# Layer norms and block sums without GpSimd: the norm's affine part as two VectorE steps, 96 GpSimd subtractions and additions moved to VectorE

## The chip, the core and the metric

The kernel runs on one core of one Trainium2 chip. The metric is the device time of one launch in microseconds (us); the time of a kernel is the median of several runs. The engines are named as in the profile: PE is TensorE (matrix products and transposes), DVE is VectorE, ACT is ScalarE, POOL is GpSimd, SP is SyncE, whose queue starts the DMAs (transfers between device memory and the on-chip SBUF). The engines run at the same time, each works through its own list of instructions in order, and they wait for each other by semaphores. PSUM is the memory that PE writes its results to.

## What is computed

One layer of a hybrid encoder on a sequence of 1024 tokens with 1024 features, everything in fp32:

```python
x = layer_norm(ALPHA * x + 0.5 * swiglu(x, ffn1_w1, ffn1_w3, ffn1_w2), ln1_g, ln1_b)
proj = x @ w_in                    # q_lat, kv_lat, k_rope, u, g_a, g_b
y_a = mla_attention(...) @ w_o_attn
y_b = s5_branch(u, ...) @ w_o_ssm
merged = sigmoid(g_a) * y_a + sigmoid(g_b) * y_b
x = layer_norm(ALPHA * x + merged @ w_out, ln2_g, ln2_b)
x = layer_norm(ALPHA * x + 0.5 * swiglu(x, ffn2_w1, ffn2_w3, ffn2_w2), ln3_g, ln3_b)
ple = sigmoid(x @ ple_w_gate) * (p @ ple_w_proj)
x = layer_norm(ALPHA * x + ple, ln4_g, ln4_b)
```

with `swiglu(x, w1, w3, w2) = (silu(x @ w1) * (x @ w3)) @ w2`, a hidden width of 2816, and

```python
def layer_norm(x, g, b):
    mu = jnp.mean(x, axis=-1, keepdims=True)
    var = jnp.mean(jnp.square(x - mu), axis=-1, keepdims=True)
    return (x - mu) * lax.rsqrt(var + LN_EPS) * g + b
```

## The kernel before

**Number format.** Each fp32 operand of a product is split into a high and a low part (`split`, L63 to L65): ACT copies the source into the rounded high part (L64), DVE subtracts it from the source (L65). A product is then three matmuls, high by high, high by low and low by high (`mm3`, L80; `prod` for the blocks of the feed-forward part). Names ending in `h` or `hi` are high parts, names ending in `l` or `lo` low parts. PE thus waits for ACT and then for DVE wherever new weights or new activations come in.

**Feed-forward up.** `ffn_up` (L274 to L336) multiplies 2x2 blocks with seven products in place of eight. The seven need sums of blocks: those of the weights are made by `sums_of` (from L253 on; tiles `c`, `shi`, `slo`, `thi`, `tlo`, `fhl`), those of the activations once, by `lead` for the first feed-forward part and by `transpose_sums` (L162 to L195) for the second; their tiles are `xah`/`xal`, `tbh`/`tbl`, `tch`/`tcl` and `td`. The loop runs over 11 pairs of column blocks in each of the two parts, 22 in all. In each, L325 and L326 form the gated hidden blocks `s1` and `s2`, and L330 to L333, on POOL, form four sums of them, `c1` and `c2`, 128x512 elements each. All go to device memory (`hd`).

**Lead.** At the start of the kernel L511 and L513 (DVE) and L520 and L521 (POOL) form block sums of the transposed input, tiles `rawx` and `t` of 128x1024, while the first products already run on the blocks that need no sum (L502).

**Feed-forward down.** `ffn_down` (L338 to L417) reads `hd` back (`raw`, split into `hh`, `hl`), splits the weights `w2` (`wh`, `wl`) and adds seven products (`pd`, `pdy`) into eight accumulators `acc`, 128 tokens by 1024 features each. At the end of each accumulator the scalar_tensor_tensor of L363 also returns the sums of its rows.

**Norms.** `layer_norm` (L113 to L140) is called 32 times, for eight tiles `acc` in each of four norms. L118 (DVE) makes the negative mean `nm`, L121 (ACT) the sum of squares about it, L122 to L128 (DVE on 128x1 and one square root on ACT) the reciprocal deviation `rs`. In 30 of the calls the affine part then follows as four steps on three engines: L137 (DVE, 128x1), L138 (ACT, 128x1024), L139 (POOL, 128x1024, times the gain), L140 (DVE, 128x1024, plus the bias). In the last two tiles of the fourth norm it is the form with two scalar_tensor_tensor steps per half, L132 and L134, and an output DMA after each half. After the first three norms PE transposes each tile (`tln`; L151 in `transpose_in`, L170 in `transpose_sums`), and ACT and DVE split the result (`xhi`, `xlo`). `norm_in` takes the tiles one by one and lets the transposes lag by two or three tiles.

In `transpose_sums`, tiles 4 to 7 of the second norm are combined with tiles 0 to 3: L184 copies one transposed tile (`xo`), L187 and L188 form `xp`, L191 and L192 `xq`, and L193, on POOL, the last difference in `xo`.

**Gate of the last stage.** L959 starts `pgate`, the product with `ple_w_gate`: 24 matmuls per tile of 128 tokens, over four weight tiles split into `whi` and `wlo`. `pproj` is the product with `ple_w_proj`; its activations are split into the tile `pq`.

**What sets the order.** The program is built with `schedule_with_timeline_sim=True` (L1413): a scheduler of the framework orders the instructions of each engine, ahead of the run, by a timeline of its own. What the diff changes in one place can thus move instructions in others; the order shown below is that of the built programs.

Of the kernel before, what the change touches and what calls it, by code (L numbers as in the profile page):

```python
# [24 lines left out]
AF = mybir.ActivationFunctionType  # L25
ALU = mybir.AluOpType
# [19 lines left out]
def layer_kernel(ctx, tc, A):  # L46
# [66 lines left out]
    def layer_norm(a, sums, gt, bt, pool, out=None):  # L113
# [15 lines left out]
        if out is not None:  # L129
            cs = [slice(c, c + 512) for c in (0, 512)]  # L130
            for c in cs:
                V.scalar_tensor_tensor(out=a[:, c], in0=a[:, c], scalar=nm, in1=gt[:, c], op0=ALU.add, op1=ALU.mult)  # L132
            for c in cs:
                V.scalar_tensor_tensor(out=a[:, c], in0=a[:, c], scalar=rs, in1=bt[:, c], op0=ALU.mult, op1=ALU.add)  # L134
                nc.sync.dma_start(out[:, c], a[:, c])
            return
        V.tensor_tensor(out=nm, in0=nm, in1=rs, op=ALU.mult)  # L137
        S.activation(a, a, AF.Identity, bias=nm, scale=rs)  # L138
        G.tensor_tensor(out=a, in0=a, in1=gt, op=ALU.mult)  # L139
        V.tensor_tensor(out=a, in0=a, in1=bt, op=ALU.add)  # L140
# [21 lines left out]
    def transpose_sums(a, j, X, pool):  # L162
# [30 lines left out]
        G.tensor_tensor(out=o[:, l], in0=o[:, r], in1=p[:, l], op=ALU.subtract)  # L193
# [80 lines left out]
    def ffn_up(fp, X, w1, w3, hd, lead):  # L274
# [32 lines left out]
        for p in range(NP):  # L307
# [22 lines left out]
            G.tensor_tensor(out=c1[:, l], in0=s1[:, r], in1=s2[:, r], op=ALU.add)  # L330
            G.tensor_tensor(out=c1[:, r], in0=c1[:, l], in1=s1[:, l], op=ALU.subtract)
            G.tensor_tensor(out=c2[:, l], in0=s1[:, l], in1=s1[:, r], op=ALU.subtract)
            G.tensor_tensor(out=c2[:, r], in0=s2[:, l], in1=c1[:, r], op=ALU.subtract)  # L333
# [124 lines left out]
    with tc.tile_pool(name="f1", bufs=1, reuse_waits="tile") as fp:  # L458
# [6 lines left out]
        def lead(banks, start):  # L465
# [41 lines left out]
            t2s = []  # L507
# [8 lines left out]
            for kp in range(2):  # L516
                k = 2 * kp
                t1, b21, b12, b22 = raws[0][kp], raws[0][kp + 2], raws[1][kp], raws[1][kp + 2]
                split(t1, tb[0][:, k + 4:k + 6, :], tb[1][:, k + 4:k + 6, :])
                G.tensor_tensor(out=b12, in0=b22, in1=b12, op=ALU.subtract)  # L520
                G.tensor_tensor(out=b21, in0=b21, in1=t2s[kp], op=ALU.subtract)  # L521
                split(b12, tcs[0][:, k:k + 2, :], tcs[1][:, k:k + 2, :])
                split(b22, tcs[0][:, k + 4:k + 6, :], tcs[1][:, k + 4:k + 6, :])
                split(b21, td[:, k:k + 2, :], td[:, k + 4:k + 6, :])
# [288 lines left out]
    gt = []  # L813
# [603 lines left out]
```

## Time and profile before

| | |
|---|---|
| time, median of 3 runs | 2406.77 us (2405.56 to 2407.76) |
| the profiled execution's own time | 2407.14 us |
| its span, first to last instruction | 2405.3 us, so 1.84 us lie around it |
| instructions in the trace | 28500 |
| busy: DVE, ACT, POOL | 1625.7, 984.0 and 623.6 us |

The stages of the span, by the profile's table of windows and its timeline: the lead to about 45 us, feed-forward up to 446, down to about 691 with the first norm in its last part, projections, S5 branch, attention and merge to 1540, the second norm to 1625, feed-forward up to 2020 and down to 2266 with the third norm, then the gate, the projection and the fourth norm to the end.

How to read the rows that follow: a row of the timeline gives the start in the span (us), the duration (us), the engine, the line of the kernel, the operation, the tile written and the tiles read, the shape, and in brackets how long the engine was idle before it and whose work ended that. DVE overlaps the end of one instruction with the start of the next, so the distance between two starts is shorter than the duration. A row of the windows gives a stretch of the span, its length, the busy time and the number of instructions of each engine, the clock granted to PE as a share of full speed, the share of the DMA engines and their GB/s.

### The profile page before, as it was taken

Reading aid. Unit: us, or ns where it says so; the run is one execution under the profiler, and the core shown is the slowest. Engines: PE = TensorE matmul, PEld = TensorE weight load, DVE = VectorE, ACT = ScalarE, POOL = GpSimd, SP = SyncE. Lnnn points to the kernel's source line nnn. Section 1 sums busy time; section 2 is a strip of 40 time slices with the busy share of each in tenths; the row PEclk is TensorE's granted clock in tenths of the full one; section 3 lists DMA queues with packets and bytes.
Section 4 is the critical chain, followed back from the end, with each engine's and each line's share of the span. In section 5 each row is a group of like instructions: output and inputs, shape, how many; then the busy total and the mean of one; then the engine's idle time right before and its main releaser. Section 6 shows DMA issues by size and latency. Waiting matters only on the chain.

```text
span 2405.3 us, 28500 instructions
## 1 busy us (share of the span) xinstructions
PE 2273.2 (95%) x10704; PEld 1867.9 (78%) x10704; DVE 1625.7 (68%) x2316; ACT 984.0 (41%) x1390; POOL 623.6 (26%) x545
## 2 busy tenths in 40 slices
PE   5999999999979989998999999969999999999898
PEld 4888888877768878886888888758888888777686
DVE  7656565775587799948688875675656556764845
ACT  4333333333442313334477871353333333333627
POOL 2111010200038555524255542220201112000302
PEclk8999999999989989999999999979999999999899
DMA  3333232842244223335100034112323236622211
GB/s 122 113 97 120 84 114 86 316 184 95 81 143 144 94 75 90 105 127 214 62 10 27 27 129 160 40 57 93 122 88 119 88 110 255 239 94 95 75 53 70
DMA packets 103898, 265.62 MB, mean 110 GB/s; under 512 B 13264, under 2 KB 27856, under 8 KB 103760
## 3 DMA queue, kind: packets, MB, share of 16 engines
q1 hardware_dynamic: 103760, 263.80, 32.1%
q8 instruction: 84, 1.38, 0.2%
q14 instruction: 54, 0.44, 0.1%
HBM read 189.33 MB, written 74.42 MB: 110 GB/s over the span
## 4 chain that ended last, share of the span: by engine, by line
PE 76%; DVE 10%; issue 5%; DMA 4%; ACT 2%; POOL 1%; SPq 0%; DVEq 0%; ACTq 0%; POOLq 0%
PE px L246 19%; PE pg L84 11%; PE py L246 10%; PE pdy L405 7%; PE pd L405 7%; PE pz L246 5%; PE ps L84 3%; PE pd L84 2%; PE pov L693 2%; PE pya L84 2%; PE tpp L680 2%; DMA w2w<-in_ffn_w_dram 2%; PE pyb L84 2%; PE pq L84 1%; DVE acc L140 1%
## 5 line engine op out<-in xcount | busy, mean ns | idle before, releaser
L139 POOL TENSOR_TENSOR acc<-acc,ln 128x1024 f32<-128x1024 f32 x30 | 79.5, 2656 | 555.6 <-ACT acc L138 554.2
L330 POOL TENSOR_TENSOR c<-s,s 128x512 f32<-128x512 f32 x22 | 30.2, 1375 | 725.7 <-DVE s L325 654.4
L65 DVE TENSOR_TENSOR wlo<-raw,whi 128x1024 fp32r<-128x1024 f32 (+4 forms) x112 | 141.6, 1268 | 80.2 <-ACT whi L64 79.0
L64 ACT ACTIVATE whi<-raw 128x1024 fp32r<-128x1024 f32 (+4 forms) x112 | 107.6, 967 | 154.9 <-PE pg L84 111.7
L84 PE MATMUL pg<-xlo,whi 128*128 128x512 f32 x416 | 164.7, 396 | 0.3 <-DVE xlo L65 0.3
L84 PE MATMUL pg<-xhi,whi 128*128 128x512 f32 x416 | 164.8, 397 | 0.1
L84 PE MATMUL pg<-xhi,wlo 128*128 128x512 f32 x416 | 163.6, 393 | 0.0
L405 PE MATMUL pd<-wl,hh 128*128 128x512 f32 x352 | 144.0, 409 | 5.9 <-DVE wl L65 5.9
L405 PE MATMUL pd<-wh,hl 128*128 128x512 f32 x352 | 140.6, 403 | 0.0
L405 PE MATMUL pd<-wh,hh 128*128 128x512 f32 x352 | 125.3, 405 | 10.5 <-ACT hh L64 5.3
L64 ACT ACTIVATE wh<-w2w 128x1024 fp32r<-128x1024 f32 x56 | 59.3, 1058 | 166.3 <-PE pd L405 84.0
L246 PE MATMUL py<-tch,fhl 128*128 128x512 f32 x352 | 116.9, 392 | 0.0
L64 ACT ACTIVATE fhl<-raw 128x512 fp32r<-128x512 f32 x44 | 27.9, 633 | 202.3 <-PE px L246 197.2
L246 PE MATMUL px<-td,thi 128*128 128x512 f32 x352 | 108.8, 390 | 0.0
L65 DVE TENSOR_TENSOR hl<-raw,hh 128x1024 fp32r<-128x1024 f32 x84 | 101.3, 1208 | 10.2 <-ACT hh L64 8.2
L667 POOL TENSOR_SCALAR P<-P,sm 128x1024 f32<-128x1024 f32 x64 | 74.7, 1168 | 115.0 <-DVE sm L666 97.2
L260 DVE TENSOR_TENSOR c<-raw 128x512 f32<-128x512 f32 x44 | 37.8, 859 | 98.4 <-PE px L246 98.4
L405 PE MATMUL pdy<-wl,hh 128*128 128x512 f32 x264 | 104.3, 395 | 0.0
L405 PE MATMUL pdy<-wh,hl 128*128 128x512 f32 x264 | 103.9, 395 | 0.0
L405 PE MATMUL pdy<-wh,hh 128*128 128x512 f32 x264 | 99.7, 395 | 0.0
L65 DVE TENSOR_TENSOR wl<-w2w,wh 128x1024 fp32r<-128x1024 f32 x56 | 69.4, 1239 | 36.6 <-ACT wh L64 36.4
L65 DVE TENSOR_TENSOR pt<-tpp,pt 128x512 fp32r<-128x512 f32 x128 | 85.6, 684 | 11.6 <-ACT pt L64 10.1
(413 smaller groups left out, 6667.1 us busy)
## 6 DMA issues: line engine op xcount, KB each, us to landing
raw<-in_ffn_w_dram SPq DMA_DIRECT2D x86, 512.0 KB, 3.7
raw<-hd SPq DMA_DIRECT2D x70, 512.0 KB, 3.3
hd<-c SPq DMA_DIRECT2D x88, 256.0 KB, 4.4
hd<-s SPq DMA_DIRECT2D x66, 256.0 KB, 2.9
w2w<-in_ffn_w_dram SPq DMA_DIRECT2D x32, 512.0 KB, 8.7
rawx<-in_xT_dram SPq DMA_DIRECT2D x16, 256.0 KB, 5.2
w2e<-in_ffn_w_dram SPq DMA_DIRECT2D x8, 512.0 KB, 8.9
acc<-in_x_dram SPq DMA_DIRECT2D x8, 512.0 KB, 9.1
```

The costliest lines, as they stand in the source:

```text
L64: S.activation(hi, src, AF.Copy)
L65: V.tensor_tensor(out=lo, in0=src, in1=hi.bitcast(F32), op=ALU.subtract)
L84: PE.matmul(out, lhsT=a, rhs=b, start=(n == 0), stop=(n == last))
L139: G.tensor_tensor(out=a, in0=a, in1=gt, op=ALU.mult)
L140: V.tensor_tensor(out=a, in0=a, in1=bt, op=ALU.add)
L246: PE.matmul(out, lhsT=x[:, ks], rhs=y[:, k, :], start=(first and n == 0), stop=(n == 11), skip_group_check=True)
L260: V.tensor_tensor(out=c[:, r], in0=r2[:, l], in1=r2[:, r], op=ALU.add)
L330: G.tensor_tensor(out=c1[:, l], in0=s1[:, r], in1=s2[:, r], op=ALU.add)
L405: PE.matmul(P[t], lhsT=x[:, ts], rhs=y[:, ws], start=(fresh and p + a == 0 and m == 0), stop=(p + a == NP - 1 and m == 2), skip_group_chec ...
L667: G.tensor_scalar(out=P, in0=P, scalar1=sm, scalar2=1.0, op0=ALU.mult, op1=ALU.mult)
L680: PE.transpose(tp[:, k * 128:k * 128 + 128], P[:, (q * 4 + k) * 128:(q * 4 + k) * 128 + 128], idt)
L693: PE.matmul(p[:, 0:256], lhsT=vt[:, k, c0:c0 + 128], rhs=pt[k // 4][b][:, k % 4, :], start=(k == 0 and b == 0), stop=(k == 7 and b == 1))
```

## The change

- `layer_norm`: the four steps L137 to L140 are replaced, in the 30 calls, by two scalar_tensor_tensor on DVE over 128x1024. The first, `(a + nm) * gain`, needs only the mean and the end of the squares on ACT; the second, `a * rs + bias`, needs `rs`. They stand at L131 and L133 of the changed file. The last two tiles keep their halves.
- `transpose_sums`: the difference in `xo` moves from POOL to DVE (4 of 128x512).
- `ffn_up`: the four sums `c1`, `c2` move from POOL to DVE (88 of 128x512).
- `lead`: the two differences per pair of blocks move from POOL to DVE (4 of 128x1024).

In all, DVE loses 60 instructions and gains 156, ACT loses 30 of 128x1024, POOL loses 126, and PE and SP issue the same numbers as before. From the norm's end on, line numbers of the changed file are lower by 5.

```diff
-        if out is not None:
-            cs = [slice(c, c + 512) for c in (0, 512)]
...
-            return
-        V.tensor_tensor(out=nm, in0=nm, in1=rs, op=ALU.mult)
-        S.activation(a, a, AF.Identity, bias=nm, scale=rs)
-        G.tensor_tensor(out=a, in0=a, in1=gt, op=ALU.mult)
-        V.tensor_tensor(out=a, in0=a, in1=bt, op=ALU.add)
+        cs = [slice(0, 1024)] if out is None else [slice(c, c + 512) for c in (0, 512)]
+        for c in cs:
+            V.scalar_tensor_tensor(out=a[:, c], in0=a[:, c], scalar=nm, in1=gt[:, c], op0=ALU.add, op1=ALU.mult)
+        for c in cs:
+            V.scalar_tensor_tensor(out=a[:, c], in0=a[:, c], scalar=rs, in1=bt[:, c], op0=ALU.mult, op1=ALU.add)
+            if out is not None:
                 nc.sync.dma_start(out[:, c], a[:, c])
...
-        G.tensor_tensor(out=o[:, l], in0=o[:, r], in1=p[:, l], op=ALU.subtract)
+        V.tensor_tensor(out=o[:, l], in0=o[:, r], in1=p[:, l], op=ALU.subtract)
...
-            G.tensor_tensor(out=c1[:, l], in0=s1[:, r], in1=s2[:, r], op=ALU.add)
-            G.tensor_tensor(out=c1[:, r], in0=c1[:, l], in1=s1[:, l], op=ALU.subtract)
-            G.tensor_tensor(out=c2[:, l], in0=s1[:, l], in1=s1[:, r], op=ALU.subtract)
-            G.tensor_tensor(out=c2[:, r], in0=s2[:, l], in1=c1[:, r], op=ALU.subtract)
+            V.tensor_tensor(out=c1[:, l], in0=s1[:, r], in1=s2[:, r], op=ALU.add)
+            V.tensor_tensor(out=c1[:, r], in0=c1[:, l], in1=s1[:, l], op=ALU.subtract)
+            V.tensor_tensor(out=c2[:, l], in0=s1[:, l], in1=s1[:, r], op=ALU.subtract)
+            V.tensor_tensor(out=c2[:, r], in0=s2[:, l], in1=c1[:, r], op=ALU.subtract)
...
-                G.tensor_tensor(out=b12, in0=b22, in1=b12, op=ALU.subtract)
-                G.tensor_tensor(out=b21, in0=b21, in1=t2s[kp], op=ALU.subtract)
+                V.tensor_tensor(out=b12, in0=b22, in1=b12, op=ALU.subtract)
+                V.tensor_tensor(out=b21, in0=b21, in1=t2s[kp], op=ALU.subtract)
```

How the built programs differ at three places, first VectorE in the lead. In the program before, from the first low part `tbl` on, to `c`, the sum of weight blocks that the next products of PE wait for:

```order
L65 TENSOR_TENSOR tbl<-rawx,tbh 128x1024
L511 TENSOR_TENSOR rawx<-rawx 128x1024
L65 TENSOR_TENSOR tbl<-t_214,tbh 128x1024
L65 TENSOR_TENSOR tcl<-rawx,tch 128x1024
L513 TENSOR_TENSOR t_219<-rawx 128x1024
L260 TENSOR_TENSOR c<-raw 128x512
L65 TENSOR_TENSOR tcl<-rawx,tch 128x1024
L287 TENSOR_TENSOR s_259<-s_259,pz 128x512
L65 TENSOR_TENSOR tcl<-rawx,tch 128x1024
L65 TENSOR_TENSOR tbl<-rawx,tbh 128x1024
L261 TENSOR_TENSOR c<-c,raw 128x512
```

The same stretch of the changed program, with L515 and L516 the moved differences; ahead of it stand L506, L508, L515, L516, the first `tbl` and L506 again:

```order
L65 TENSOR_TENSOR tbl<-t_214,tbh 128x1024
L65 TENSOR_TENSOR tcl<-rawx,tch 128x1024 x3
L508 TENSOR_TENSOR t_219<-rawx 128x1024
L515 TENSOR_TENSOR rawx<-rawx 128x1024
L255 TENSOR_TENSOR c<-raw 128x512
L65 TENSOR_TENSOR td<-rawx,td 128x1024
L282 TENSOR_TENSOR s_259<-s_259,pz 128x512
L65 TENSOR_TENSOR tbl<-rawx,tbh 128x1024
L516 TENSOR_TENSOR rawx<-rawx,t_219 128x1024
L65 TENSOR_TENSOR tbl<-t_219,tbh 128x1024
L256 TENSOR_TENSOR c<-c,raw 128x512
```

From the first L511 (L506) on, 12 instructions of 128x1024 or 128x512 stood ahead of `c<-c,raw`; now 18 do: the four moved ones, one `td` and the second `tbl<-t` are the added ones.

Next, VectorE at the start of the gate's product after the third norm (`wlo` are the low parts of the weights that `pgate` waits for; the `ln` tiles belong to tiles 4 to 7 of the norm). Before, from the last sum of the feed-forward part on:

```order
L363 SCALAR_TENSOR_TENSOR acc,sums<-acc,pd 128x512
L137 TENSOR_TENSOR ln_17252<-ln_17252,ln_17256 128x1
L118 TENSOR_SCALAR ln_17372<-sums 128x1
L65 TENSOR_TENSOR xlo<-tln,xhi 128x8x128
L124 RECIPROCAL ln_17295<-ln_17293 128x1
L65 TENSOR_TENSOR wlo<-raw,whi 128x1024
L125 TENSOR_TENSOR ln_17293<-ln_17295 128x1
L65 TENSOR_TENSOR wlo<-raw,whi 128x1024
```

The changed program from its last such sum (L358) on:

```order
L358 SCALAR_TENSOR_TENSOR acc,sums<-acc,pd 128x512
L65 TENSOR_TENSOR wlo<-raw,whi 128x1024
L124 RECIPROCAL ln_17215<-ln_17213 128x1
L65 TENSOR_TENSOR wlo<-raw,whi 128x1024
L118 TENSOR_SCALAR ln_17326<-sums 128x1
L122 TENSOR_SCALAR ln_17290<-ln_17289 128x1
L131 SCALAR_TENSOR_TENSOR acc<-acc,ln_17288,ln 128x1024
L124 RECIPROCAL ln_17253<-ln_17251 128x1
L125 TENSOR_TENSOR ln_17213<-ln_17215 128x1
L122 TENSOR_SCALAR ln_17328<-ln_17327 128x1
L131 SCALAR_TENSOR_TENSOR acc<-acc,ln_17326,ln 128x1024
```

The `xlo` of an earlier tile now stands before the sum, and the first new norm step of all four tiles comes ahead of the second (L133), which follows for the four tiles in a row after the next two `wlo`.

Last, PE at the same place: `tln` are the transposes of tiles 4 and 5. Before, from the 18th matmul of `pgate` for its first tile of tokens on (a second row of eight transposes comes three matmuls later, ahead of `pproj`):

```order
L84 MATMUL pgate<-whi,xlo 128x512
L151 MATMUL tln<-idt,acc 128x128 x8
L84 MATMUL pgate<-whi,xhi 128x512
L84 MATMUL pgate<-wlo,xhi 128x512
L84 MATMUL pgate<-whi,xlo 128x512
```

In the changed program, from the 22nd of these matmuls on:

```order
L84 MATMUL pgate<-whi,xhi 128x512
L84 MATMUL pgate<-wlo,xhi 128x512
L84 MATMUL pgate<-whi,xlo 128x512
L146 MATMUL tln<-idt,acc 128x128 x16
L84 MATMUL pproj<-whi,pq 128x512
L84 MATMUL pproj<-wlo,pq 128x512
```

Both rows of transposes now come after all 24 matmuls of the first tile of `pgate`; before, the first stood behind the 18th.

More of the change, by code (lines that the diff above doesn't have):

```diff
@@ L128, in layer_norm @@
         V.tensor_tensor(out=rs, in0=y, in1=sq, op=ALU.mult)
-        if out is not None:
-            cs = [slice(c, c + 512) for c in (0, 512)]
[L131 to L134, printed above, removed]
-                nc.sync.dma_start(out[:, c], a[:, c])
-            return
-        V.tensor_tensor(out=nm, in0=nm, in1=rs, op=ALU.mult)
-        S.activation(a, a, AF.Identity, bias=nm, scale=rs)
-        G.tensor_tensor(out=a, in0=a, in1=gt, op=ALU.mult)
-        V.tensor_tensor(out=a, in0=a, in1=bt, op=ALU.add)
+        cs = [slice(0, 1024)] if out is None else [slice(c, c + 512) for c in (0, 512)]
[4 more added lines that the diff above has]
+            if out is not None:
+                nc.sync.dma_start(out[:, c], a[:, c])
     def transpose_in(a, j, xT, late):
```

## The prediction

> **What bounds the kernel now.** I read the page first: the busy times, then the chain that ended last.
>
> ```profile
> PE 2273.2 (95%) x10704; PEld 1867.9 (78%) x10704; DVE 1625.7 (68%) x2316; ACT 984.0 (41%) x1390; POOL 623.6 (26%) x545
> PE 76%; DVE 10%; issue 5%; DMA 4%; ACT 2%; POOL 1%; SPq 0%; DVEq 0%; ACTq 0%; POOLq 0%
> L139 POOL TENSOR_TENSOR acc<-acc,ln 128x1024 f32<-128x1024 f32 x30 | 79.5, 2656 | 555.6 <-ACT acc L138 554.2
> ```
>
> PE is the bound, and DVE has the next share of the chain. POOL holds 1%, though a norm's pass there takes 2656 ns. So the change can gain only where PE waits, and the second view was the windows, stage by stage.
>
> ```profile
> 238.00:315.50 77.50, 77.50 (x338) 63.16 (x337) 44.73 (x51) 25.53 (x34) 11.73 (x8) 1.00 0.32 102
> 649.00:725.00 76.00, 59.68 (x266) 47.40 (x265) 63.32 (x129) 40.74 (x58) 23.54 (x15) 0.89 0.36 122
> 1540.00:1625.00 85.00, 61.53 (x271) 49.21 (x270) 67.53 (x143) 45.12 (x62) 26.23 (x13) 0.83 0.14 53
> 2223.00:2300.00 77.00, 65.08 (x274) 51.52 (x274) 67.17 (x119) 45.68 (x61) 22.19 (x8) 0.89 0.31 99
> 2300.00:2394.00 94.00, 93.50 (x413) 76.16 (x411) 42.58 (x109) 49.44 (x63) 15.65 (x6) 1.00 0.08 31
> ```
>
> In the up loop (first row, two pairs) PE is busy for all 77.50 us at the full clock. In the three norm stages it lacks 16, 23 and 12 us, at a lower mean clock, with DVE at 79 to 87%. In the last 94 us, where the fourth norm runs, it lacks 0.5. The lead is the fourth place with gaps. From the second half of the first norm to the second norm's beginning (S5, attention, merge) the order of PE is the same in both programs, and I give that stretch nothing.
>
> **The lead.** The timeline of DVE and PE:
>
> ```profile
> 14.36 1.22 DVE L511 TENSOR_TENSOR rawx<-rawx 128x1024 f32<-128x1024 f32 x1
> 16.75 3.43 DVE L65 TENSOR_TENSOR tbl<-rawx,tbh 128x1024 fp32r<-128x1024 f32 x1
> 23.41 1.21 DVE L65 TENSOR_TENSOR tbl<-t,tbh 128x1024 fp32r<-128x1024 f32 x1
> 29.57 3.36 DVE L65 TENSOR_TENSOR tcl<-rawx,tch 128x1024 fp32r<-128x1024 f32 x1
> 35.72 0.68 DVE L261 TENSOR_TENSOR c<-c,raw 128x512 f32<-128x512 f32 x1
> 41.47 1.21 DVE L65 TENSOR_TENSOR slo<-c,shi 128x1024 fp32r<-128x1024 f32 x1
> 15.66 3.44 POOL L520 TENSOR_TENSOR rawx<-rawx 128x1024 f32<-128x1024 f32 x1 [14.37 <-DVE rawx L511]
> 37.55 0.79 PE L246 MATMUL px<-tbh,shi 128*128 128x512 f32 x1 [17.91 <-ACT shi L64]
> 42.73 0.79 PE L246 MATMUL px<-tbh,slo 128*128 128x512 f32 x1 [3.12 <-DVE slo L65]
> ```
>
> Of two DVE instructions of one shape, the one at 23.41 takes 1.21 us, the one at 16.75, beside the POOL row, 3.43. Four in this stretch are long by 2.2 us (the first and the last are shown), one for each POOL instruction. They end when POOL's does: 15.66 + 3.44 = 19.10, plus one undisturbed 1.1, is 20.2, and 16.75 + 3.43 is 20.18. So DVE stands still meanwhile, and the four moved instructions, at 1.21 us (1.14 from start to start), replace 8.8 us of that. By the order of the changed program 16 instructions of 128x1024 and two of 128x512 now stand between 14.36 and `c<-c,raw`: 16 x 1.14 + 2 x 0.60 = 19.4, so it starts at 33.8 instead of 35.72, and PE's wait of 17.91 us ends 1.9 us earlier. Then three of 128x512 and two of 128x1024 stand ahead of `slo`: 33.8 + 3 x 0.60 + 2 x 1.14 = 37.9 instead of 41.47, and PE's second wait ends **3.6 us** earlier. The bounds are 1.9 (`slo` gains no more than `c`) and 4.5.
>
> **The up loop.** The price of a moved sum and what stands behind it:
>
> ```profile
> 190.77 1.22 DVE L325 SCALAR_TENSOR_TENSOR s<-s,e 128x1024 f32<-128x1024 f32 x1
> 194.48 0.68 DVE L260 TENSOR_TENSOR c<-raw 128x512 f32<-128x512 f32 x1
> 195.08 1.78 DVE L65 TENSOR_TENSOR fhl<-raw,fhl 128x512 fp32r<-128x512 f32 x1
> 196.78 1.78 DVE L261 TENSOR_TENSOR c<-c,raw 128x512 f32<-128x512 f32 x1
> 201.23 0.39 PE L246 MATMUL py<-tch,fhl 128*128 128x512 f32 x1
> ```
>
> A 128x512 costs 0.60 from start to start, so the 88 moved sums add 88 x 0.60 = 53 us to DVE. What hides them is DVE's idle 32.8 of 77.5 us and a lead: `fhl` ends at 196.86, PE takes it at 201.23, 4.4 us later. Per pair DVE gains four sums, 2.4 us, two of them ahead of `fhl`, and loses two stretches of 1.1 beside POOL (195.08, 196.78). The cost is **0**. Were the cover gone, it would be up to 22 x 2.4 = 53 us, but `fhl` comes only 2 x 0.60 - 1.1 = 0.1 later than now. The DMAs of the sums (`hd<-c`) are issued by SP in the same order, a little earlier. The ends of the loop, where PE waits for `hd` to come back, move with it: 0, bounds -1 and +1.
>
> The row at 190.77 also prices the new norm steps: 1.22 us for a scalar_tensor_tensor of 128x1024, like L140's 1.21. A tile loses L140 and L137 on DVE and gains two of these, 1.07 us more from start to start.
>
> **The first norm.**
>
> ```profile
> 653.33 0.34 DVE L118 TENSOR_SCALAR ln<-sums 128x1 f32<-128x1 f32 x2
> 654.58 0.16 DVE L125 TENSOR_TENSOR ln<-ln 128x1 f32<-128x1 f32 x1
> 658.13 2.18 DVE L128 TENSOR_TENSOR ln<-ln,ln 128x1 f32<-128x1 f32 x1
> 660.42 1.22 DVE L65 TENSOR_TENSOR wl<-w2w,wh 128x1024 fp32r<-128x1024 f32 x1
> 691.58 0.69 DVE L363 SCALAR_TENSOR_TENSOR acc<-acc,pd 128x512 f32<-128x512 f32 x1 [0.22 <-PE pd L405]
> 703.33 1.94 PE L151 MATMUL tln<-idt,acc 128*128 128x128 f32 x8 [11.78 <-DVE acc L140]
> ```
>
> Here too a step of one element per row takes 2.18 us beside POOL where its neighbours take 0.16. In the new order three L131 and one L133 stand between 653.33 and `wl`, with one accumulation and some nine small steps: 4 x 1.14 + 0.60 + 9 x 0.16 = 6.6, so `wl` starts at 659.9 instead of 660.42. PE also does tile 0's eight transposes in this gap (1.94 us at the low clock of the row at 703.33, half of it at the full one). Together the products end about 1.4 us earlier. For tile 4 no pass on ACT and POOL is left; but the last accumulation (at 691.58, so now at 690.2), three L131, two `wlo` and about 17 small steps stand ahead of its L133: 690.2 + 0.6 + 5 x 1.14 + 17 x 0.14, then the L133 itself with 1.2, gives 700.1 for the transposes in place of 703.33. **3.3 us**, bounds 1 (the small steps cost 0.28 each) and 5.5 (they fill waits).
>
> **The second norm.**
>
> ```profile
> 1550.13 0.69 DVE L233 SCALAR_TENSOR_TENSOR acc<-acc,pd 128x512 f32<-128x512 f32 x1
> 1551.44 2.17 DVE L125 TENSOR_TENSOR ln<-ln 128x1 f32<-128x1 f32 x1
> 1577.76 0.80 PE L246 MATMUL px<-xah,whi 128*128 128x512 f32 x1 [0.96 <-ACT xah L64]
> 1592.41 0.69 DVE L187 TENSOR_TENSOR xp<-tln,xo 128x512 f32<-128x512 f32 x1 [2.03 <-PE tln L170]
> 1594.95 1.40 DVE L65 TENSOR_TENSOR tbl<-xp,tbh 128x1024 fp32r<-128x1024 f32 x1 [1.12 <-ACT tbh L64]
> ```
>
> From the accumulation at 1550.13 to the point where tile 3 can be transposed, the new order has ten instructions of 1.14 (L131 and L133 of four tiles, two `xal`), seven accumulations of 0.60 and about 28 small steps of 0.12: 19.0, so 1569.1; transposes and two copies of 1.0 on ACT lead to 1572 for the products that now start at 1577.76. Part of that is lost, since the last two L133 then wait for `pz` in DVE's list; I take 5 at L187. The chain of tiles 4 to 7 keeps its length: the moved subtraction, 0.60, falls into the 1.12 us in which DVE waits for `tbh`. **5.0 us**, bounds 2 and 7.
>
> **The third norm.**
>
> ```profile
> 2235.74 0.79 PE L405 MATMUL pd<-wl,hh 128*128 128x512 f32 x1 [1.66 <-DVE wl L65]
> 2236.00:2244.00 8.00, 8.00 (x27) 6.34 (x28) 7.97 (x13) 2.99 (x4) 3.03 (x1) 0.63 0.45 121
> 2266.49 0.69 DVE L363 SCALAR_TENSOR_TENSOR acc<-acc,pd 128x512 f32<-128x512 f32 x1 [0.41 <-PE pd L405]
> 2275.97 1.91 PE L151 MATMUL tln<-idt,acc 128*128 128x128 f32 x8 [3.33 <-DVE acc L140]
> 2280.29 1.21 DVE L65 TENSOR_TENSOR wlo<-raw,whi 128x1024 fp32r<-128x1024 f32 x1
> 2281.56 0.79 PE L84 MATMUL pgate<-wlo,xhi 128*128 128x512 f32 x1 [3.25 <-DVE wlo L65]
> 2285.41 0.78 PE L84 MATMUL pproj<-whi,pq 128*128 128x512 f32 x1
> ```
>
> The start is that of the first norm, 1.4 earlier, so the last accumulation comes at 2265.1. Behind it stand two `wlo`, two L131 and seven small steps (0.60 + 4 x 1.14 + 1.1), and about 0.4 of waiting for ACT's squares, before the fourth `wlo`: 2271.8 instead of 2280.29. PE's wait at 2281.56 thus goes; what is late next is tile 4, whose L133 ends at about 2276.3, almost when it is transposed now, but behind all 24 matmuls. Transposes, the ACT copies `xhi` and `pq` at 1.0 each, and `pproj` starts at about 2280.2 instead of 2285.41. I take off 0.7 for a lower clock there: **4.5 us**, bounds 1.5 and 7. The fourth norm lies under busy PE, and the two tiles behind the last matmul have the old form: 0.
>
> **Sum.** 3.6 + 3.3 + 5.0 + 4.5 = 16.4 from the profiled execution's 2407.14 is **2390.7**; its time is 0.4 above the median of the runs. All lower bounds leave 2400.7, all upper ones 2383.1.
>
> **Rivals.**
>
> *DVE becomes the norms' bound* (slower). Place: the DVE lists of the three norm stages and the lead. It decides if the 2.2 us stretches don't go with POOL's work, because DVE's own operands cause them. Then `wl` comes 4 us later in the first and the third norm (four steps of 1.14, less 0.6 that falls in waits), tile 4 another 1.5, the lead loses 4 x 1.14 = 4.6: 2407 + 2 x 5.5 + 4.6 = 2423. For it: DVE is busy for 67.17 of 77 us in the third stage, and 8 x 1.07 = 8.6 us come on top. Against it: in the rows shown, every stretch lies beside a POOL instruction and ends with it.
>
> The Trainium skill, Perfetto Trace Analysis, section Optimizing Scalar/DVE Operations, says that a saturated VectorE is a reason to hand work to ScalarE or even GpSimd, the opposite of this change, and adds that this may not help, since GpSimd and VectorE share a read port. By the first half the stage would get up to 8.6 us longer; the stretched rows bear out the second half, and I go by them.
>
> *The gains sit in front of other waits.* Each restart runs into the transfers or the lower clock: only the lead's 1.9 and 2 us per norm remain, or less, down to none: 2399 to 2407, likeliest 2400. For it: behind the wait of 3.33 us at 2275.97 stands one of 3.25 at 2281.56, so one goes and the next can take its place. Against it: the up loop behind the lead has no gap into which its gain could fall.
>
> *The clock holds.* After two waits of PE, of which the row at 2235.74 ends the second with 1.66 us, the granted clock is 0.63 for 8 us, a loss of 8 x 0.37 = 3.0. With the transposes in that gap the clock may stay up, in the first and the third norm: 2390.7 - 6.0 = 2384.7. Against it: the waits are short now, and the clock falls all the same.
>
> The Trainium skill, TensorE: Matmul & The Clock Gate, section Part 1: The HAM clock gate, has the clock drop only after an idle window of about 3.4 us. By that rule the present waits would not lower it; the window row does not agree, so I keep the lower clock in the sum.
>
> **How the numbers follow.** Forecast 0.66 (2383 to 2398), clock 0.13, other waits 0.15, DVE bound 0.06. A measurement of this kernel can tell about 0.2%, 4.8 us, so faster means below 2402: the forecast, the clock, and a little over half of other waits, 0.87; same 0.08; slower 0.05. The range reaches from 2382 to 2402: it takes in both sums of bounds and the clock, and leaves out the DVE bound and the upper end of other waits.
>
> **What would show it.** In the changed profile: no DVE instruction of 128x1024 above 1.5 us in the lead and the norms; PE's restarts near 35.6 and 39.1; the up loop's windows still fully busy; the transposes of tile 4 of the first norm near 696.5 (700.1 less the lead's 3.6); the first `pproj` some 17 us ahead of 2285.4. The forecast is wrong if PE gaps appear in the up loop, if the stretches stay, or if the waits at the norms keep their length under another name.

## The result and the profile after

| | before | changed |
|---|---|---|
| median of 4 runs each, on one chip | 2406.16 us (2402.98 to 2407.76) | 2385.43 us (2381.87 to 2387.60) |
| the profiled execution, and its span | 2407.14, 2405.3 us | 2386.72, 2384.9 us |

The ratio is 0.9914 with a 95% interval of 0.9897 to 0.9931: 20.7 us less, where 16.4 were forecast. The time lies in the range, and the direction and the place of the gain are those of the forecast. The sizes of three terms are not, and part of the agreement of the sum is that their errors have opposite signs.

The page of the changed kernel, its busy times and its chain that ended last:

```profile
PE 2265.6 (95%) x10704; PEld 1863.9 (78%) x10704; DVE 1602.7 (67%) x2412; ACT 952.4 (40%) x1360; POOL 388.5 (16%) x419
PE 82%; DVE 8%; DMA 4%; ACT 3%; issue 2%; POOL 1%; SPq 0%; DVEq 0%; ACTq 0%
```

DVE executes 96 instructions more than before (2412 against 2316), the added ones all with 512 or 1024 elements per row, and is busy for 23.0 us **less**. POOL's share of the chain was 1% before and is 1% now; PE's rose from 76 to 82%, and those of DVE and of issue fell. What POOL cost stood under DVE's name.

The windows of the same five stretches, each shifted to the place where its work now lies (two pairs of the up loop, the three norms, the last stage):

```profile
235.00:312.50 77.50, 77.50 (x337) 63.11 (x336) 43.77 (x58) 25.72 (x35) 0.00 (x0) 1.00 0.32 102
646.00:722.00 76.00, 62.70 (x293) 50.38 (x292) 58.52 (x150) 33.01 (x51) 5.59 (x23) 0.93 0.34 123
1537.00:1622.00 85.00, 65.59 (x311) 54.18 (x310) 71.57 (x147) 41.63 (x62) 0.00 (x0) 0.86 0.17 62
2206.00:2283.00 77.00, 67.86 (x295) 53.41 (x294) 61.49 (x122) 39.86 (x55) 0.00 (x0) 0.93 0.32 101
2290.00:2373.00 83.00, 83.00 (x360) 67.83 (x360) 44.54 (x101) 38.05 (x50) 0.00 (x0) 1.00 0.10 39
```

The up loop is as full as before, and DVE needs 43.77 us there, with seven instructions more, in place of 44.73. In each norm stage PE does more matmuls in the same width, at a higher mean clock: 0.93, 0.86 and 0.93 in place of 0.89, 0.83 and 0.89.

To see where the 20.4 us of the span went, I compare the time at which the same PE instruction starts in both traces. The difference is the gain so far:

| up to | gain so far | the stage's part | forecast |
|---|---|---|---|
| the lead's second restart | 3.8 | 3.8 | 3.6 |
| the down part, behind its first products | 3.3 | -0.5 | 0 (-1 to +1) |
| the first norm's products all running | 9.2 | 5.9 | 3.3 (1 to 5.5) |
| the last products before the second norm | 6.8 | -2.4 | 0 |
| the second up loop | 16.7 | 9.9 | 5.0 (2 to 7) |
| the last matmul | 20.6 | 3.9 | 4.5 (1.5 to 7) |
| the end of the span | 20.4 | -0.2 | 0 |

**Lead and up loop.** The timeline of DVE and PE:

```profile
18.73 1.22 DVE L65 TENSOR_TENSOR tbl<-rawx,tbh 128x1024 fp32r<-128x1024 f32 x1
33.55 0.68 DVE L256 TENSOR_TENSOR c<-c,raw 128x512 f32<-128x512 f32 x1
37.63 1.22 DVE L65 TENSOR_TENSOR slo<-c,shi 128x1024 fp32r<-128x1024 f32 x1
35.38 0.79 PE L241 MATMUL px<-tbh,shi 128*128 128x512 f32 x1 [16.44 <-ACT shi L64]
38.90 0.79 PE L241 MATMUL px<-tbh,slo 128*128 128x512 f32 x1 [1.45 <-DVE slo L65]
189.20 0.69 DVE L65 TENSOR_TENSOR fhl<-raw,fhl 128x512 fp32r<-128x512 f32 x1
```

The first `tbl` takes 1.22 us where it took 3.43. `c` starts at 33.55 (forecast 33.8), `slo` at 37.63 (37.9), PE at 35.38 and 38.90 (35.6 and 39.1). In the up loop `fhl` takes 0.69 us, not 1.78. In the lead and the three norm stages no DVE instruction of 128x1024 takes more than 1.5 us now; twelve did before, so the stretches are gone where the prediction looked for that.

**First norm.** PE's waits and what DVE does ahead of the second:

```profile
653.83 1.06 PE L146 MATMUL tln<-idt,acc 128*128 128x128 f32 x8 [0.45 <-DVE ln L122]
658.00 0.50 PE L400 MATMUL pd<-wl,hh 128*128 128x512 f32 x1 [1.98 <-DVE wl L65]
695.41 1.94 PE L146 MATMUL tln<-idt,acc 128*128 128x128 f32 x8 [10.35 <-DVE ln L128]
691.87 1.27 DVE L131 SCALAR_TENSOR_TENSOR acc<-acc,ln,ln 128x1024 f32<-128x1024 f32 x1
694.00 1.27 DVE L133 SCALAR_TENSOR_TENSOR acc<-acc,ln,ln 128x1024 f32<-128x1024 f32 x1
685.00:696.00 11.00, 0.65 (x4) 0.62 (x4) 11.00 (x34) 5.35 (x12) 0.00 (x0) 0.64 0.27 95
```

Tile 4's transposes start at 695.41, where the prediction named 696.5. The wait before them is still 10.35 us (11.78 before), and DVE is busy for all 11.00 us of the last row: the wait is now DVE's list, with the L131 of later tiles ahead of the L133 that PE waits for.

The granted clock behind the two waits, first of the program before, then of the changed one, at the beginning of the norm and behind tile 4's wait:

```profile
662.00:670.00 8.00, 8.00 (x34) 6.49 (x34) 7.96 (x13) 4.19 (x5) 3.05 (x1) 0.82 0.60 187
702.00:714.00 12.00, 10.67 (x40) 8.89 (x41) 8.92 (x10) 2.15 (x2) 6.06 (x7) 0.70 0.40 163
```

```profile
658.00:666.00 8.00, 8.00 (x34) 6.51 (x35) 8.00 (x23) 4.04 (x7) 0.00 (x0) 1.00 0.38 131
694.00:706.00 12.00, 10.59 (x46) 9.00 (x47) 6.19 (x10) 1.02 (x1) 0.00 (x0) 0.82 0.69 256
```

In the first place the clock stays at 1.00: 8 x 0.18 = 1.4 us. In the second it comes back sooner, 12 x (0.82 - 0.70) = 1.4 us. Together 2.8, and the term came out 2.6 above its forecast. The first half of it is chance, as the rows under the third norm show.

**Second norm.** PE's restarts, the steps of tiles 4 to 7, and the clock, in the changed program and, in the last row, in the one before:

```profile
1564.25 0.50 PE L241 MATMUL px<-xah,whi 128*128 128x512 f32 x1 [1.16 <-ACT xah L64]
1577.31 0.69 DVE L182 TENSOR_TENSOR xp<-tln,xo 128x512 f32<-128x512 f32 x1 [2.15 <-PE tln L165]
1579.85 1.23 DVE L65 TENSOR_TENSOR tbl<-xp,tbh 128x1024 fp32r<-128x1024 f32 x1 [0.40 <-ACT tbh L64]
1605.73 0.80 PE L241 MATMUL px<-tbh,slo 128*128 128x512 f32 x1 [0.38 <-DVE slo L65]
1564.00:1578.00 14.00, 13.75 (x72) 11.57 (x72) 11.71 (x29) 4.27 (x9) 0.00 (x0) 1.00 0.37 150
```

```profile
1577.80:1591.40 13.60, 13.60 (x50) 10.96 (x51) 7.58 (x18) 5.22 (x7) 6.24 (x3) 0.80 0.19 79
```

The first product starts 1577.76 - 1564.25 = 13.5 us earlier; 6.8 of it were there already, so the stage has gained 6.7 at this point (forecast 5.8). Behind it the clock is 1.00, not 0.80. The same 48 products took 13.5 us and take 11.9 now, although eight transposes (0.8 us) now stand among them (the higher count in the row, 72 against 50, is due to transposes). At `xp` the gain is 1592.41 - 1577.31 = 15.1, at `slo` 16.0.

**Third norm and end.**

```profile
2219.56 0.50 PE L400 MATMUL pd<-wl,hh 128*128 128x512 f32 x1 [1.99 <-DVE wl L65]
2220.00:2228.00 8.00, 8.00 (x30) 6.34 (x29) 8.00 (x23) 3.71 (x7) 0.00 (x0) 0.79 0.41 131
2256.09 1.23 DVE L65 TENSOR_TENSOR wlo<-raw,whi 128x1024 fp32r<-128x1024 f32 x1 [0.62 <-ACT whi L64]
2257.38 0.50 PE L84 MATMUL pgate<-wlo,xhi 128*128 128x512 f32 x1 [0.77 <-DVE wlo L65]
2265.28 0.50 PE L84 MATMUL pproj<-whi,pq 128*128 128x512 f32 x1 [0.35 <-ACT pq L64]
```

The fourth `wlo` starts 24.2 us earlier (2280.29 before), but PE takes little of that: `pproj` starts 20.1 us earlier, 3.4 more than the second up loop had. The clock at the start of this norm is 0.79, not 0.63, but it does fall, behind a wait of 1.99 us, while behind the first norm's of 1.98 it stays at 1.00.

The traces' clock records tell why. In all 14 traces of this case (before, changed, e1 to e12) the granted clock is 1.00 or 0.50, and it changes only at points of a grid of 3.41 us, which lies elsewhere in every execution. The start of the third norm, cut on that grid, first in the changed kernel's trace and then in that of e9, the same kernel with PE's instructions in the same order:

```profile
2217.36:2220.77 3.41, 1.42 (x6) 1.03 (x6) 3.41 (x5) 2.90 (x5) 0.00 (x0) 1.00 0.00 0
2220.77:2224.18 3.41, 3.41 (x9) 2.64 (x9) 3.41 (x5) 1.24 (x2) 0.00 (x0) 0.50 0.66 191
```

```profile
2215.31:2218.72 3.41, 1.73 (x9) 0.97 (x7) 3.41 (x6) 3.41 (x6) 0.00 (x0) 1.00 0.00 0
2218.72:2222.14 3.42, 3.13 (x13) 2.55 (x14) 3.42 (x6) 2.24 (x4) 0.00 (x0) 1.00 0.32 66
```

With PE busy for 1.42 of 3.41 us the next stretch runs at 0.50; with 1.73 it runs at 1.00. At the first norm it is the other way round: 1.97 us busy and 1.00 behind it here, 1.43 us and 0.50 in e9. Over the 14 traces, every grid stretch at full clock in which PE was busy for less than 44% was followed by the half clock, none above 61% was, and in between both occur. So whether a wait of 2 us costs a half-speed stretch (half of 3.41, so 1.7 us) depends on where it falls on the grid, and that is chance. No run moved the grid; this is read off the traces.

### The profile page after: what moved, and what is told of

It reads as the page before. It is cut to its first block, busy times and chain, and to the rows that moved or that the text cites. A ratio compares the mean times of both kernels' runs of the same rounds, so it can differ in the third digit from the quotient of the medians.

```text
span 2384.9 us, 28380 instructions
## 1 busy us (share of the span) xinstructions
PE 2265.6 (95%) x10704; PEld 1863.9 (78%) x10704; DVE 1602.7 (67%) x2412; ACT 952.4 (40%) x1360; POOL 388.5 (16%) x419
## 4 chain that ended last, share of the span: by engine, by line
PE 82%; DVE 8%; DMA 4%; ACT 3%; issue 2%; POOL 1%; SPq 0%; DVEq 0%; ACTq 0%
PE px L241 19%; PE pg L84 11%; PE py L241 10%; PE pdy L400 8%; PE pd L400 7%; PE pz L241 5%; PE pd L84 4%; PE pgate L84 3%; PE ps L84 3%; PE pov L688 2%; PE pya L84 2%; PE tpp L675 2%; DMA w2w<-in_ffn_w_dram 2%; PE pyb L84 2%; PE pq L84 1%
## 5 line engine op out<-in xcount | busy, mean ns | idle before, releaser
L255 DVE TENSOR_TENSOR c<-raw 128x512 f32<-128x512 f32 x44 | 30.3, 689 | 113.9 <-PE px L241 113.9
L65 DVE TENSOR_TENSOR hl<-raw,hh 128x1024 fp32r<-128x1024 f32 x84 | 94.9, 1131 | 11.3 <-ACT hh L64 11.2
L65 DVE TENSOR_TENSOR wl<-w2w,wh 128x1024 fp32r<-128x1024 f32 x56 | 68.4, 1221 | 39.1 <-ACT wh L64 38.9
L241 PE MATMUL px<-tbh,shi 128*128 128x512 f32 x176 | 70.8, 402 | 23.6 <-ACT shi L64 23.6
```

The costliest lines, as they stand in the source:

```text
L65: V.tensor_tensor(out=lo, in0=src, in1=hi.bitcast(F32), op=ALU.subtract)
L241: PE.matmul(out, lhsT=x[:, ks], rhs=y[:, k, :], start=(first and n == 0), stop=(n == 11), skip_group_check=True)
L255: V.tensor_tensor(out=c[:, r], in0=r2[:, l], in1=r2[:, r], op=ALU.add)
```

## The experiments

All times are medians; each ratio is to the kernel before, from runs on the same chip, with its 95% interval. The kernels of one group shared the runs of the kernel before: e1 to e4, e5 to e8, e9 to e12. Where an edit is a part of the change's diff as it stands, words name the part.

**The parts of the change alone.** e1 is the kernel before with the lead's two lines alone:

```diff
-                G.tensor_tensor(out=b12, in0=b22, in1=b12, op=ALU.subtract)
-                G.tensor_tensor(out=b21, in0=b21, in1=t2s[kp], op=ALU.subtract)
+                V.tensor_tensor(out=b12, in0=b22, in1=b12, op=ALU.subtract)
+                V.tensor_tensor(out=b21, in0=b21, in1=t2s[kp], op=ALU.subtract)
```

e2 has the four lines of `ffn_up` alone, the first of them:

```diff
-            G.tensor_tensor(out=c1[:, l], in0=s1[:, r], in1=s2[:, r], op=ALU.add)
+            V.tensor_tensor(out=c1[:, l], in0=s1[:, r], in1=s2[:, r], op=ALU.add)
...
```

e3 has both and the line of `xo` (all the moved sums) with the old norm, and e4 the diff's part in `layer_norm` and nothing else.

> Only the four sums of the lead move to VectorE (the norms, c1/c2 and xo stay as before). Theory (GpSimd's work makes VectorE stand still): PE's second restart comes at about 38.9 as in the changed kernel (42.73 before), and the 3.8 us last to the end: ratio 0.998, some 2402.5 us. Rival (what the lead gains is lost at the transfers behind the up loop): restart near 38.9 too, but the end within 1.5 us of before.

> Only the 88 sums c1, c2 move to VectorE. Theory: no PE gap in the up loop before or after, so the time stays within 1.5 us of before, ratio 0.9995 to 1.0005; VectorE's busy time in two pairs stays at 44 to 45 us, because 4.8 us of sums come and 4.4 us of standing still go. Rival (VectorE's list gets longer and its splits reach PE late): PE gaps in the up loop, 1 us or more per pair, over 2420 us.

> The lead, c1/c2 and xo move to VectorE, the norms stay in four steps on three engines. Theory: 3.8 us of the lead and about 0.5 to 1 us of xo, ratio 0.998, some 2402 us. Rival (the moved block sums of the second norm's stage carry half of that stage's 10.5 us): 2397 us.

> Only the norm's affine part changes; the lead, c1/c2 and xo stay on GpSimd. Theory: the three norm stages give 6, 10 and 4.5 us, with some 3 us lost in the middle if that loss belongs to the norms' change and not to the run: 2386 to 2390 us, ratio 0.992 to 0.994. Rival (the order of the scheduler, not the norm's steps, brings the stages' gains): another sum than 20.7 less what the lead and the sums bring alone.

| | us | ratio |
|---|---|---|
| e1, lead | 2400.69 | 0.9982 (0.9973 to 0.9991) |
| e2, up loop | 2405.61 | 1.0004 (0.9995 to 1.0013) |
| e3, all sums | 2401.43 | 0.9978 (0.9969 to 0.9986) |
| e4, norm | 2389.54 | 0.9929 (0.9917 to 0.9942) |
| the change | 2385.43 | 0.9914 (0.9897 to 0.9931) |

The parts add up: 0.0022 for the sums and 0.0071 for the norm make 0.0093, against 0.0086 together. The lead's gain is there in full, and stays to the end: e1 has 3.6 to 4.8 us along nearly all of its trace. The 88 sums of the up loop cost nothing. The window of e2:

```profile
238.00:315.50 77.50, 77.50 (x337) 63.09 (x337) 43.76 (x58) 25.69 (x35) 0.00 (x0) 1.00 0.32 102
```

DVE is busy there for 43.76 us, less than the 44.73 of before: what it gains in sums it gets back in stretches. So about four fifths of the gain are the norms'.

**Merged steps, or steps off POOL?** e5 is the changed kernel with the old four steps, the multiplication by the gain on DVE instead of POOL:

```diff
...
-        for c in cs:
-            V.scalar_tensor_tensor(out=a[:, c], in0=a[:, c], scalar=nm, in1=gt[:, c], op0=ALU.add, op1=ALU.mult)
...
+        V.tensor_tensor(out=nm, in0=nm, in1=rs, op=ALU.mult)
+        S.activation(a, a, AF.Identity, bias=nm, scale=rs)
+        V.tensor_tensor(out=a, in0=a, in1=gt, op=ALU.mult)
+        V.tensor_tensor(out=a, in0=a, in1=bt, op=ALU.add)
```

> All sums on VectorE as in the changed kernel, but the norm's affine part in its old four steps, with the multiplication by the gain on VectorE instead of GpSimd: ScalarE's scaled pass, then two passes of VectorE. Theory A (what counts is that GpSimd no longer holds VectorE and is out of the chain): nearly the whole gain, 2386 to 2390 us. Theory B (what counts is that the first of the two steps can run before the deviation is known, and that ScalarE is out of the chain): half of the norms' gain is missing, 2394 to 2398 us.

2388.89 us, 0.9931 (0.9919 to 0.9944): 0.0069 of the changed kernel's 0.0086. Most of the gain needs no merged step; that POOL has left the norm (and the sums, 0.0022 in e3) is enough. What the merge itself adds, 0.0017, is not separated by the intervals. e5 takes away two things at once, POOL's pass in the chain of each tile and its reading beside DVE. How the gain divides between them no run tells; the next three look at the second alone.

**POOL beside the norm again.** Three kernels give POOL one instruction of 128x1024 per norm (30 in all) that writes a scratch tile nobody reads. Only a later tile's squares, which ACT writes to the same tile, could wait for it; they did for 1.4 us in all in e6, and for less than 1 us in e11. They differ in what POOL reads. One tile, in e6:

```diff
         V.tensor_tensor(out=rs, in0=y, in1=sq, op=ALU.mult)
+        if out is None:
+            G.tensor_scalar(out=scratch, in0=gt, scalar1=nm, scalar2=None, op0=ALU.mult)
```

> The changed kernel, and in each of 30 norms GpSimd multiplies the gain by the negative mean into the scratch tile of the squares, which nobody reads afterwards; only the next but one tile's squares wait for it. Theory (a GpSimd instruction that reads SBUF holds VectorE instructions with two SBUF operands until it ends): VectorE instructions of the norm stages are long again, by up to GpSimd's 1.2 us each, and the kernel loses 3 to 10 us of its gain, 2388 to 2395 us. Rival (the standing still belongs to the chain through the tile, not to the work beside it): 2385 us, no long instruction.

Two tiles, in e11, at the same place:

```diff
+            G.tensor_tensor(out=scratch, in0=gt, in1=bt, op=ALU.add)
```

> The changed kernel, and in each of 30 norms GpSimd adds the gain and the bias (two fp32 operands in SBUF, 128x1024, as L139 had) into the scratch tile of the squares; nobody reads the sum. Theory (a GpSimd instruction with two SBUF operands holds VectorE until it ends): VectorE instructions of the norm stages take 3 us and more again, three or four in each half norm, and 6 to 14 us of the gain are lost, 2391 to 2399 us. Rival (as with the one-operand instruction: VectorE is held by 0.3 to 0.8 us and GpSimd waits instead): 3 us lost, 2388 us.

Nothing, in e12:

```diff
+            G.memset(scratch, 0.0)
```

> The changed kernel, and in each of 30 norms GpSimd sets the scratch tile of the squares to zero, which reads nothing from SBUF; nobody reads the zeros. Theory (only GpSimd's reads hold VectorE): no VectorE instruction is long, and the time is that of the changed kernel within 2 us, but for squares that wait for GpSimd. Rival (the loss of 3 us with the one-operand instruction came from those waiting squares): 3 us lost here too.

| POOL reads | us | ratio |
|---|---|---|
| one tile (e6) | 2387.79 | 0.9927 (0.9914 to 0.9941) |
| two tiles (e11) | 2432.58 | 1.0114 (1.0100 to 1.0128) |
| nothing (e12) | 2383.71 | 0.9917 (0.9903 to 0.9930) |

e6 was a miss: it cost some 3 us at most, far from giving the gain back. The groups of e6, of e11 and of e12 (busy time and mean ns of one), with single instructions:

```profile
L130 POOL TENSOR_SCALAR scr<-ln,ln 128x1024 bf16<-128x1024 f32 x30 | 104.2, 3478 | 1421.8 <-ACT scr L121 1419.0 <-ACT ln L123 1.8 <-DVE ln L126 1.0
L133 DVE SCALAR_TENSOR_TENSOR acc<-acc,ln,ln 128x1024 f32<-128x1024 f32 x30 | 44.4, 1480 | 0.0
648.24 2.85 POOL L130 TENSOR_SCALAR scr<-ln,ln 128x1024 bf16<-128x1024 f32 x1 [646.95 <-ACT scr L121]
648.59 1.84 DVE L133 SCALAR_TENSOR_TENSOR acc<-acc,ln,ln 128x1024 f32<-128x1024 f32 x1
2325.00 1.29 DVE L133 SCALAR_TENSOR_TENSOR acc<-acc,ln,ln 128x1024 f32<-128x1024 f32 x1
2325.03 3.89 POOL L130 TENSOR_SCALAR scr<-ln,ln 128x1024 bf16<-128x1024 f32 x1 [67.15 <-ACT scr L121]
```

```profile
L130 POOL TENSOR_TENSOR scr<-ln 128x1024 bf16<-128x1024 f32 x30 | 85.9, 2877 | 1475.8 <-ACT scr L121 1475.8
L133 DVE SCALAR_TENSOR_TENSOR acc<-acc,ln,ln 128x1024 f32<-128x1024 f32 x30 | 75.3, 2511 | 0.0
648.15 2.40 POOL L130 TENSOR_TENSOR scr<-ln 128x1024 bf16<-128x1024 f32 x1 [646.85 <-ACT scr L121]
648.51 3.12 DVE L133 SCALAR_TENSOR_TENSOR acc<-acc,ln,ln 128x1024 f32<-128x1024 f32 x1
696.82 6.46 DVE L65 TENSOR_TENSOR wlo<-raw,whi 128x1024 fp32r<-128x1024 f32 x2
```

```profile
L130 POOL MEMSET scr<- 128x1024 bf16 x30 | 28.5, 951 | 1487.1 <-ACT scr L121 1487.0
L133 DVE SCALAR_TENSOR_TENSOR acc<-acc,ln,ln 128x1024 f32<-128x1024 f32 x30 | 38.3, 1276 | 0.0
686.12 0.95 POOL L130 MEMSET scr<- 128x1024 bf16 x1 [23.52 <-ACT scr L121]
686.17 1.27 DVE L133 SCALAR_TENSOR_TENSOR acc<-acc,ln,ln 128x1024 f32<-128x1024 f32 x1
```

Beside two inputs on POOL the first norm step on DVE (L133 in these files) rises from 1276 to 2511 ns, single ones to 3.50 us, and two `wlo`, which have nothing to do with the norm, take 6.46. Beside a memset it stays at 1276, also where the two lie on top of each other (686.12 and 686.17). So it is POOL's **reading** that holds DVE, not its being there. (DVE's instructions stand in almost the same order in e11 and e12; 7 of 2412 differ.)

How long it holds DVE depends on what it reads. In e11 the POOL row at 648.15 comes first, and DVE's step, 1.27 us by itself, ends 3.12 us after 648.51: it was held until 2.21 us after POOL's start (648.51 + 3.12 - 1.27 - 648.15), nearly all of POOL's 2.40. In e6, with one input, the same sum gives 648.59 + 1.84 - 1.27 - 648.24 = 0.92 us, and the four other pairs of this kind in e6, with no other such step of DVE under way, give 0.92 or 0.93 too. Where DVE starts first or at the same time, as at 2325.00, DVE is not held (1.29 us), and POOL takes 3.89 us in place of 2.85. POOL's 2.85 is no sign of waiting: none of e6's thirty takes less than 2.84, also where no such step of DVE overlaps it. So e6 is cheap because each hold is short and because DVE often comes first.

The Trainium skill, SBUF — State Buffer, section Who interferes with whom, says that a VectorE instruction with two SBUF inputs contends with a GpSimd instruction that reads SBUF, not with one that only writes. e11 (2511 ns) and e12 (1276 ns) agree. It adds that the order of issue decides which of the two waits; the two pairs of e6 agree (POOL first: 2.85 and 1.84 us; DVE first: 1.29 and 3.89).

**The shape and the place of the two steps.** In e7 both steps run in halves of 512 columns in all norms:

```diff
-        cs = [slice(0, 1024)] if out is None else [slice(c, c + 512) for c in (0, 512)]
+        cs = [slice(c, c + 512) for c in (0, 512)]
```

> The changed kernel with both norm steps in halves of 512 columns in all 32 norms. VectorE's time is nearly the same (four of 0.6 us for two of 1.2 us). Theory (the transposes wait for the whole tile, since eight of them read it in one go and the last four need the second half): within 1.5 us of the changed kernel. Rival (finer pieces let PE begin 0.6 us sooner at each of the stages): 2 us faster.

In e8 an extra step of 128x1 rewrites `nm` from `rs` and itself, without changing its value, so that the first step can't run before the tile's `rs` is there:

```diff
         V.tensor_tensor(out=rs, in0=y, in1=sq, op=ALU.mult)
+        if out is None:
+            V.tensor_scalar(out=nm, in0=rs, scalar1=0.0, scalar2=nm, op0=ALU.mult, op1=ALU.add)
```

> The changed kernel with one more step of 128x1 that rewrites the negative mean after the deviation is known, so that no first step (a + nm) * gain can be put ahead of another tile's chain. Theory (tile 4's transposes now wait behind the first steps of tiles 5 to 7 in VectorE's list, 3.6 us): the wait ahead of these transposes in the first norm falls from 10.35 us to 8 or 9, and the kernel gains 1 to 3 us on the changed one. Rival (the first steps only fill time in which VectorE would wait for ScalarE): the chain of each tile gets longer by 1.2 us, and the kernel loses 1 to 5 us.

e9 is the changed kernel again, for the third group. In e10 the step of e8 stands in the first three norms only, those that `norm_in` calls:

```diff
...
+        if turn:
+            V.tensor_scalar(out=nm, in0=rs, scalar1=0.0, scalar2=nm, op0=ALU.mult, op1=ALU.add)
...
-            layer_norm(acc[j], sums, gt, bt, pool)
+            layer_norm(acc[j], sums, gt, bt, pool, turn=True)
```

> The changed kernel itself, beside the next three on the same chip: ratio 0.9914 within its interval of 0.9897 to 0.9931, some 2385 us. If the part of the gain beyond the forecast was chance, 0.993 or more.

> As the kernel with the late first step, but only in the first three norms, whose tiles are transposed; the fourth norm is that of the changed kernel. Theory (the late step gains at tile 4 of the first and the third norm, and loses 3.3 us behind the last matmul, where tile 5's two steps stand in front of the last two tiles): ratio 0.988 to 0.9895, 2377 to 2380 us, 5 to 8 us below the changed kernel. Rival (the end is late because PE came earlier and something else holds it): 2381 to 2383 us, as with all four norms.

| | us | ratio |
|---|---|---|
| e7, halves | 2389.14 | 0.9929 (0.9916 to 0.9942) |
| e8, first step held back, all norms | 2381.79 | 0.9901 (0.9886 to 0.9915) |
| e9, changed kernel | 2384.72 | 0.9915 (0.9901 to 0.9928) |
| e10, held back, three norms | 2381.90 | 0.9903 (0.9890 to 0.9917) |

Halves gain nothing; e7 is some 3.6 us above the changed kernel by the ratios, more than the 1.5 expected, with intervals that overlap. Holding the first step back shortens the wait that is late now, as the row of e8 for tile 4 of the first norm shows:

```profile
690.59 1.94 PE L148 MATMUL tln<-idt,acc 128*128 128x128 f32 x8 [7.45 <-DVE acc L135]
```

7.45 us in place of 10.35: the L131 of later tiles no longer stand ahead of the L133 that PE waits for. In e8's trace 3.5 us of the gain are lost again behind the last matmul, in the fourth norm; e10 was to get them back. It does so in its trace (last matmul 26.7 us and end of the span 26.2 us ahead of before), but its median is that of e8, and the expectation missed. Both are some 3 us below the changed kernel, with intervals that overlap. Side by side on one chip, though, all four runs of e10 (2380.97 to 2382.43) lie below all four of e9 (2383.09 to 2385.53). So they are the likely fastest versions, by a margin that is near what can be told apart here.

## Why the prediction was right, and where not

- **The cause.** The argument was that DVE's long instructions beside POOL are POOL's doing and go with it. Shown: e11 brings them back at the new place, e12 does not, and e5 has most of the gain from taking POOL out alone. Not shown is how much of that gain comes from the stretches and how much from the shorter chain of each tile. The rival by which DVE becomes the norms' bound (2423) needed the stretches to stay; they went, and DVE's busy time fell.
- **Lead**: 3.8 against 3.6, each restart within 0.3 us of its forecast time, and e1 alone gives 0.0018, or 4.3 us.
- **Up loop**: 0, as forecast, in e2 and in the windows. The transition to the down part lost 0.5, inside its bounds of 1.
- **First norm, mis-sized**: 5.9 against 3.3, above the upper bound of 5.5. The step that failed is the one that left the clock as it was; without the clock's part, 2.8, the stage comes out at 3.1. The rival "the clock holds" put 3.0 on this stage, for one stretch at its beginning; half of the 2.8 lies there and half behind tile 4's wait, where the forecast had no term. The half at the beginning is luck: e9, the same kernel, has the clock at 0.50 there, and this stage gives 4.6. The wait ahead of tile 4, 11.78 us before, is still 10.35, close to the prediction's own sign of being wrong, a wait that keeps its length under another name.
- **Second norm, mis-sized**: 9.9 against 5.0, above the upper bound of 7. The rival had no clock term here, and this was the clock's largest place: 13.6 x (1.00 - 0.80) = 2.7 us, read off the windows; e9 has no half clock at this point either. The rest is the first product, 0.9 earlier than worked out, and the loss of 0.8 that I took off for the last L133 and that did not come. DVE's wait for `tbh`, 1.12 us before, is 0.40 with the moved subtraction ahead of it.
- **Middle, mis-sized**: -2.4 where I wrote nothing, because PE's order is the same in both programs. The order is, the waits are not, and at a few places the shift shrinks: where PE waits for DVE in the S5 branch; around 1104 us, where two waits trade lengths; and around 1135, by 1.3, where the clock differs:

```profile
1135.00:1146.00 11.00, 9.11 (x39) 6.76 (x38) 9.69 (x11) 4.35 (x7) 7.20 (x4) 1.00 0.29 109
```

```profile
1127.00:1139.00 12.00, 10.16 (x37) 7.65 (x36) 9.83 (x11) 5.12 (x8) 7.21 (x4) 0.86 0.32 115
```

  The first row is before, the second after: 1.00 against 0.86 over 12 us. But e9 loses 1.0 at the same place with the clock at 1.00, so the clock is not the whole cause. Over the middle e3 and e9 lose 2.4 us, e4 1.5, and e5, e6, e8, e10 and e11 2.8 to 4.2; e1, e2 and e12 lose nothing and e7 0.3. No run tried why, and it stays open. This is what the rival "the gains sit in front of other waits" described, at a place that I had written off.
- **Third norm**: 3.9 against 4.5. In e9's trace, the same kernel, this stage gives 7.5; one trace can't size it better than that. Half of the difference arises in the down part ahead of the norm (a loss of 0.9 here, a gain of 0.9 there), the other half, 1.8, in the norm, where one half-speed stretch of the clock is worth 1.7. That tile 4's L133 would be late next was right: PE's wait for the fourth `wlo` has fallen from 3.25 to 0.77 us, and `pproj` gains 3.4, not the 24.2 - 16.7 = 7.5 of `wlo`.
- **End**: 0, as forecast.
- **The sum.** 2.6 and 4.9 us too little in two norms, 2.4 and 0.5 too much in the middle and at the transition: that the total is only 4 us off is in part luck. The likeliest case held; about 5.5 us of clock came on top (1.4 + 1.4 + 2.7), and about 3 went off to other waits. The measured time lies nearer to the clock rival's 2384.7 than to 2390.7, but not by that rival's account: it put 3.0 each on the first and the third norm, where the windows give 2.8 and 8 x (0.79 - 0.63) = 1.3, and nothing on the second, where they give 2.7. The sums of the bounds, 2400.7 and 2383.1, leave out the up loop's -1 and +1; with them they are 2401.7 and 2382.1, still inside the range.
- **What of the clock is shown.** That the clock differs, and by how much, is read off the windows; that the place of a wait on the 3.41 us grid decides it is shown by two traces of the same kernel. That the shorter waits of this change make the half clock rarer on the whole is argued, since no run changed the waits and nothing else.

The Trainium skill, TensorE: Matmul & The Clock Gate, section Part 1: The HAM clock gate, has the clock drop only after an idle window of about 3.4 us. The grid of 3.41 us agrees with that length. But the clock fell behind a stretch in which PE was busy for 1.42 of 3.41 us, so the stretch need not be idle.

## What to carry to other kernels

Look in the timeline for DVE instructions that take two or three times the duration of others of their shape, and at what POOL reads at that moment: an elementwise pass with two inputs on POOL can hold DVE for nearly its whole length (2.21 of 2.40 us here), so that moving it to DVE can make DVE's own busy time shorter. Then price the granted clock as a term of its own at every wait that gets shorter, with a share of chance (1.7 us for each stretch here), and do not write off a stretch because its order is unchanged; its waits come at other times. Once an engine's list is the wait, look for work of later tiles that stands ahead of the step the bound engine is waiting for: holding it back shortened that wait from 10.35 to 7.45 us here.

## What had not been expected of the hardware

- Thirty POOL instructions with two inputs and no reader cost 2432.58 - 2384.72 = 48 us, 1.6 us each and more than the whole change gained; 6 to 14 had been expected. DVE's busy time rises from 1602.5 us in e9 to 1656.7 in e11, by 54 us, while POOL's new work is 85.9.
- The same thirty with one input cost 3 us at most, though POOL is busy longer with them (104.2 us): each holds DVE until 0.92 us after its start instead of 2.21, and only where POOL comes first.
- Executions of one kernel that agree within 0.2% in all can differ by 3 us in a single stage: 3.9 and 7.5 us for the third norm, in the traces of two executions of the changed kernel. A good part of that is where the waits fall on the clock's 3.41 us grid.
